# One decoder trunk on one core: the last token block's last 512 columns in two halves of 256, and the other blocks' output transfers issued by SP alone

## The chip, the cores and the metric

The kernel runs on one core of one Trainium2 chip. The metric is the device time of one execution in microseconds (us). Before the change three runs took 1270.3, 1270.86 and 1270.3 us, so the median is 1270.3 us. The execution that the profiler recorded took 1270.41 us by the same clock; the span in its trace, from the first to the last instruction, is 1268.6 us, so 1.8 us lie outside the trace.

## The reference: what is computed

Two layers over 512 tokens of 1024 numbers: a convolution module and a retention module, each followed by a feed-forward block with a short causal convolution. Everything is float32. What matters here is the very end:

```python
def conv_ffn(x, w_in, dw_w, dw_b, w_out):
    h = x @ w_in
    a, u = jnp.split(h, 2, axis=-1)
    a = causal_dwconv(a, dw_w, dw_b)
    return (jax.nn.silu(a) * u) @ w_out
...
        x = x + conv_ffn(h, ffn_w_in[i], ffn_dw_w[i], ffn_dw_b[i], ffn_w_out[i])
    return rmsnorm(x, final_g)
```

The last product, `@ w_out` of layer 1, gives 512 x 1024 numbers. They are added to the residual x, and each token's row is divided by the root of the mean of its 1024 squares and multiplied by the gain final_g. A token's scale is known only when its whole row is.

## The kernel before

**Precision.** A float32 product is made of three matmuls: each operand is split into a high part (rounded by ScalarE, line 238 or 384) and the rest (VectorE, lines 242 and 385), and `mm3` (lines 307 to 310) adds high by high, low by high and high by low in one PSUM bank. So lines 308, 309 and 310 carry the matmuls of nearly all stages; the tile names tell the stage.

**Order of work.** The layer's feed-forward block runs in four groups of hidden columns (line 30). For each group the hidden values `ys` are made first, and then they are multiplied by `w_out` (loop at line 1334). That second product is laid out with tokens on the partitions: for each half g of the 1024 output columns (g = 0 is columns 0 to 511, g = 1 is 512 to 1023) and each of the four blocks tb of 128 tokens, one PSUM bank `lo` takes 128 x 512 results. The last group has four hidden tiles (y_18 to y_21), so a bank of it takes 4 x 3 = 12 matmuls of 512 columns, and for g = 1 these come for all four tb in turn from one chunk of weights. A scheduler that works from a model of the engines sets the order of the instructions within each engine's queue; each engine then runs its queue strictly in order.

**The tail.** `finish` (line 1312) is called for each bank. In the last group it does, for block tb and half g:

- line 1318, VectorE: bank plus residual into `xT[2*tb+g]`;
- line 1321, ScalarE: the squares of it, with their sum per token into `ssq` (a second instruction reads the accumulator);
- for g = 0: line 1323, VectorE: sum/1024 + 1e-6; line 1324, GpSimd: the half is multiplied by the gain (`fgb[0]`, the tile `cos` reused);
- for g = 1: line 1327, VectorE: the two sums together into `fv`; line 1328 calls `rsqrt_small` (line 346), which raises `fv` to the power -0.5 on GpSimd (line 350) into `fr`; line 1329, ScalarE: the half g = 0 times `fr`; line 1330, ScalarE's queue: the output transfer of that half (128 rows of 2 KB, 256 KB); line 1331, VectorE: the half g = 1 times `fr` times the gain (the tile `sin`); line 1332, SP's queue: its output transfer (256 KB).

So there are eight output transfers, four issued by ScalarE and four by SP, all at the end. Below, C0 to C3 stand for line 1329 of blocks 0 to 3, M0 to M3 for line 1331, and Q3 for line 1321 of block 3 and g = 1.

`ssq` lives in the pool `sp` of small tiles. Pools lie one behind the other in SBUF, each tile rounded up to 32 bytes, so the pools opened after `sp` (the split activations and the working tiles of each stage) start where `sp` ends.

Of the kernel before, what the change touches and what calls it, by code (L numbers as in the profile page):

```python
# [9 lines left out]
F32 = mybir.dt.float32  # L10
F32R = mybir.dt.float32r
I32 = mybir.dt.int32
AF = mybir.ActivationFunctionType
ALU = mybir.AluOpType
PSUM = bass.MemoryType.PSUM

P = 128
D = 1024
S = 512
KD = D // P  # L20
NTB = S // P
# [134 lines left out]
def trunk(ctx, tc, xt_d, positions, ret_gn_g, final_g, weights_d, cols_d, mats_d, ident_d, decay_d, invf_d, out):  # L156
    nc = tc.nc
    pe, act, dve, pool = nc.tensor, nc.scalar, nc.vector, nc.gpsimd
# [3 lines left out]
    xp = ctx.enter_context(tc.tile_pool(name="xp", bufs=1))  # L162
    sp = ctx.enter_context(tc.tile_pool(name="sp", bufs=4))
# [6 lines left out]
    def psum(name):  # L170
        return pp.tile([P, S], F32, tag="ps", name=name)
# [135 lines left out]
    def mm3(ps, wh, wl, xh, xl, first, last, **check):  # L307
        pe.matmul(ps, wh, xh, start=first, stop=False, **check)  # L308
        pe.matmul(ps, wl, xh, start=False, stop=False, **check)  # L309
        pe.matmul(ps, wh, xl, start=False, stop=last, **check)  # L310
# [33 lines left out]
    xT = [xs_all[:, k, :] for k in range(KD)]  # L344
# [73 lines left out]
    QB = 32  # L418

    def blocks(t):  # L420

        return t.rearrange("p (a b q) -> p a b q", a=NTB, q=QB)
# [449 lines left out]
    N2 = S // 2  # L872
# [112 lines left out]
    def ffn_half(fp, l, norm, f0, f1, hooks=(), side=None, each=None):  # L985
        ys, wt, mid = [], {}, {}
        hooks = list(hooks)

        def mm(f):
            if f % 2 == 0:  # L990
                wt["a"] = weights()
                wt["u"] = weights()
            o = (f % 2) * P
            mid[f] = []
            for which in "au":
                ps = psum(f"f{which}{l}_{f}")
                for k in range(KD):
                    mm3(ps, *wt[which](k, o, o + P), *norm.xs[k], k == 0, k == KD - 1)
                mid[f].append(ps)
                hook = hooks.pop(0) if hooks else None  # L1000
                if hook:
                    hook()

        def evac(f):
            pa, pu = mid.pop(f)
            ap = fp.tile([P, S + 32], F32, tag="ap", bufs=2, name=f"ap{l}_{f}")[:, :2 + S]
            pool.memset(ap[:, :2], 0.0)
            dve.tensor_tensor(out=ap[:, 2:], in0=pa, in1=norm.rb, op=ALU.mult)  # L1008
            t = taps(fp, l, f, ap)
            scaled = pool.tensor_tensor(out=t, in0=t, in1=norm.rb, op=ALU.mult)  # L1010
            y = fp.tile([P, S], F32, tag="fy", bufs=2, name=f"fy{l}_{f}")
            product = dve.tensor_tensor(out=y, in0=pu, in1=t, op=ALU.mult)
            ys.append(split(y, f"y{l}_{f}", ("yh", "yl"), fp))
            if side is not None and f >= 2:
                with tc.issue_after(scaled.ins), tc.issue_after(product.ins):
                    next(side, None)

        mm(f0)
        for f in range(f0 + 1, f1):
            mm(f)  # L1020
            evac(f - 1)
            if each is not None:
                next(each, None)
        evac(f1 - 1)
        return ys

    with ExitStack() as es:
# [4 lines left out]
        def sums_of_x():  # L1032

            yield
            for k in range(4):
                left.sums_of(k)
                yield

        for n, (f0, f1, by_blocks) in enumerate(GROUPS[0]):
            if by_blocks:  # L1040
                ys = ffn_blocks(fp, 0, n1, f0, f1, left, rot)
            else:
                ys = ffn_half(fp, 0, n1, f0, f1, (None, n1.stats, n1.bcast), each=sums_of_x())
# [9 lines left out]
    with ExitStack() as es:  # L1053
# [191 lines left out]
        def ret_y(h, yt):  # L1245
            if h == H - 1:
                ys = []
                for e in range(4):
                    ps = psum(f"yt{h}{e}")
                    for i in range(NTB):  # L1250
                        pe.transpose(ps[:, i * P:(i + 1) * P], yt[i][:, e * P:(e + 1) * P], ident)
                    ys.append(split(ps, f"yt{h}{e}", ("yth", "ytl"), rt4))
                return ys
            return [split(yt[:, e], f"yt{h}{e}", ("yth", "ytl"), rt4) for e in range(4)]
# [3 lines left out]
        v = ret_vg(0, 0)  # L1258
# [11 lines left out]
        for h in range(1, H):  # L1270
            qk, ys = ret_qk(h, yt)
            proj_out(ys, f"ro{h - 1}", None, order=by_quarter, groups=(0,) if h == H - 1 else (0, 1))
            sc = ret_scores(h, qk, None)
            v, gg = ret_vg_blocks(h)
# [3 lines left out]
        ys = ret_y(H - 1, yt)  # L1278
# [4 lines left out]
    with ExitStack() as es:  # L1283
        fp = es.enter_context(tc.tile_pool(name="f1", reuse_waits="tile", bufs=6))
        lp = es.enter_context(tc.tile_pool(name="lp", reuse_waits="tile", bufs=1))
        xt = lp.tile([P, NTB, 4, KD * QB], F32, name="xt")
        sum_pool[0] = fp
        fgb = (cos, sin)
        for g in range(2):
            act.dma_start(fgb[g], final_g[512 * g:512 * (g + 1)].partition_broadcast(P))  # L1290
        lefts = []

        def between():


            xq = fp.tile([P, 4, NTB, KD, QB], F32, tag="sh", bufs=1, name="xq")
            for k in range(KD):
                dve.transpose(xq[:, :, :, k, :].rearrange("p c t q -> p t c q"), blocks(xT[k]))
            yield
            quarters(xt, xq.rearrange("p c t k q -> p c t (k q)"), nc.sync)  # L1300
            left = Factors(n3, list(n3.xs), fp, lambda name: fp.tile([P, 2, N2], F32, tag="fy", bufs=2, name=name), True)
            lefts.append(left)
            for k in range(4):
                left.sums_of(k)
                if k < 3:
                    yield
            for k in range(KD):
                left.normed_split(k)

        ssq = sp.tile([P, NTB, 2], F32, tag="ssq", bufs=1, name="ssq")  # L1310

        def finish(n, g, tb, ps):
            d = xt[:, tb].rearrange("p a (k q) -> p k a q", q=QB)[:, 4 * g:4 * g + 4]
            if n < len(GROUPS[1]) - 1:
                dve.tensor_tensor(out=d, in0=blocks(ps), in1=d, op=ALU.add)
                return
            dv, d = d, xT[2 * tb + g]
            dve.tensor_tensor(out=blocks(d), in0=blocks(ps), in1=dv, op=ALU.add)
            j = xp.tile([P, S], F32, tag="nsq", bufs=2, name=f"junk{tb}{g}")
            v = ssq[:, tb, g:g + 1]  # L1320
            act.activation(j, d, AF.Square, accum_out=v)
            if g == 0:
                dve.tensor_scalar(out=v, in0=v, scalar1=1.0 / D, scalar2=EPS, op0=ALU.mult, op1=ALU.add)
                pool.tensor_tensor(out=d, in0=d, in1=fgb[0], op=ALU.mult)
                return
            vv = sp.tile([P, 1], F32, tag="fv", name=f"fv{tb}")
            dve.tensor_scalar(out=vv, in0=v, scalar1=1.0 / D, scalar2=ssq[:, tb, 0:1], op0=ALU.mult, op1=ALU.add)
            r = rsqrt_small(vv, 1, f"fr{tb}")
            act.activation(xT[2 * tb], xT[2 * tb], AF.Copy, scale=r)
            nc.scalar.dma_start(out[0, tb * P:(tb + 1) * P, :512], xT[2 * tb])  # L1330
            dve.scalar_tensor_tensor(out=d, in0=d, scalar=r, in1=fgb[1], op0=ALU.mult, op1=ALU.mult)
            nc.sync.dma_start(out[0, tb * P:(tb + 1) * P, 512:], d)

        for n, (f0, f1, by_blocks) in enumerate(GROUPS[1]):
            if by_blocks:
                ys = ffn_blocks(fp, 1, n3, f0, f1, lefts[0])
            else:
                side = between()
                ys = ffn_half(fp, 1, n3, f0, f1, (None, n3.stats, n3.bcast), each=side)
                for _ in side:  # L1340
                    pass
            nk = len(ys)
            for g in range(2):
                last = n == len(GROUPS[1]) - 1 and g == 1
                ps = [psum(f"lo{n}{g}{tb}") for tb in range(NTB)]
                groups = []
                for k0, kn in _out_chunks(f0, f1, last):
                    groups += [(k0 + k, k, w) for w in [weights()] for k in range(kn)]
                    if last and k0 + kn < nk and k0 > 0:
                        continue  # L1350
                    for tb in range(NTB):
                        for f, k, w in groups:
                            yh, yl = ys[f]
                            mm3(ps[tb], yh[:, tb * P:(tb + 1) * P], yl[:, tb * P:(tb + 1) * P], *w(k, 0, 512),
                                f == 0, f == nk - 1)
                        if k0 + kn == nk:
                            finish(n, g, tb, ps[tb])
                    groups = []
# [79 lines left out]
```

## Time and profile before

| | |
|---|---|
| median of three runs | 1270.3 us |
| profiled execution | 1270.41 us |
| its span | 1268.6 us |
| instructions | 17818 |
| TensorE busy | 1257.9 us, 99% of the span |
| VectorE busy | 949.8 us, 75% |
| ScalarE busy | 617.5 us, 49% |
| GpSimd busy | 269.0 us, 21% |
| mean granted TensorE clock | 0.998 |
| output transfers of 256 KB | 4 on ScalarE's queue, 4 on SP's, median 3.1 us from issue to landing |

Times in the trace are in us from the span's start. PE is TensorE, PEld its weight load, DVE VectorE, ACT ScalarE, POOL GpSimd, SP the engine that only issues transfers; a name with q (ACTq, SPq) is that engine's queue issuing something. q1 is the hardware queue of the transfers that SP issues, q10 that of ScalarE's; both are served by the same 16 DMA engines. A row of the timeline gives start, duration, engine, line, what is written and read, and in brackets the idle time before it and what ended it. An instruction's duration includes its way through the pipeline, so the next may start on the same engine before it ends.

### The profile page before, as it was taken

The numbers are of one execution on the slowest core, as the hardware profiler recorded it, in microseconds if no ns is written. First come the engines' busy times: TensorE is split into PE (matmuls) and PEld (weight loads), VectorE is DVE, ScalarE is ACT, GpSimd is POOL, SyncE is SP. The second block draws the span as 40 slices with busy tenths as digits, with TensorE's granted clock in tenths as the row PEclk, the third lists the DMA queues.
The fourth block names the chain that finished last, engine by engine and source line by source line (L and its number), as shares of the span: only waits on it lengthen the run. The fifth ranks groups of instructions, "written<-read, shape, count | busy, mean of one in ns | idle before, by whom it ended". The sixth has DMA issues, their size and how long they took to land.

```text
span 1268.6 us, 17818 instructions
## 1 busy us (share of the span) xinstructions
PE 1257.9 (99%) x7035; PEld 1099.1 (87%) x7035; DVE 949.8 (75%) x1346; ACT 617.5 (49%) x900; POOL 269.0 (21%) x242
## 2 busy tenths in 40 slices
PE   9999999999999999999999999999999999999997
PEld 7889988888998998888888888878888899899896
DVE  6998757884796798589696696596879677577565
ACT  6646644442562665435335345344536256266354
POOL 0958321011101110221311412304312100010002
PEclk9999999999999999999999999999999999999999
DMA  8633332233655664313314404313152664565531
GB/s 328 237 126 108 112 120 77 103 121 100 175 158 133 184 151 164 116 67 108 108 42 154 135 27 166 116 74 134 67 149 86 160 170 143 140 169 153 128 100 67
DMA packets 38100, 164.26 MB, mean 129 GB/s; under 512 B 4992, under 2 KB 11904, under 8 KB 24192
## 3 DMA queue, kind: packets, MB, share of 16 engines
q1 hardware_dynamic: 27936, 134.01, 30.2%
q0 software_dynamic: 6480, 23.60, 10.2%
q10 hardware_dynamic: 3600, 5.52, 1.5%
q8 instruction: 55, 0.90, 0.3%
q14 instruction: 29, 0.24, 0.1%
HBM read 137.94 MB, written 2.10 MB: 110 GB/s over the span
## 4 chain that ended last, share of the span: by engine, by line
PE 95%; DVE 3%; issue 1%; POOL 1%; DMA 0%; ACT 0%; SPq 0%; POOLq 0%; DVEq 0%
PE fz L310 5%; PE fz L309 5%; PE fz L308 5%; PE fo L308 3%; PE fo L309 3%; PE fo L310 3%; PE lo L308 3%; PE lo L309 3%; PE lo L310 3%; PE cph L621 3%; PE qk L308 2%; PE qk L309 2%; PE qk L310 2%; PE fp L309 2%; PE fp L308 2%; PE fp L310 2%
## 5 line engine op out<-in xcount | busy, mean ns | idle before, releaser
L242 DVE TENSOR_TENSOR wl<-wr,wh 128x1024 fp32r<-128x1024 f32 (+2 forms) x272 | 334.0, 1233 | 143.5 <-ACT wh L238 140.8
L238 ACT CAST wh<-wr 128x1024 fp32r<-128x1024 f32 (+2 forms) x274 | 281.7, 1032 | 284.5 <-PE lo L309 49.3
L1116 POOL TENSOR_TENSOR gg<-gg,gn 128x512 f32<-128x512 f32 x16 | 27.5, 1721 | 179.3 <-ACT gg L1115 179.3
L670 DVE SCALAR_TENSOR_TENSOR tp<-hp,prm,tp 128x512 f32<-128x512 f32 x80 | 55.7, 745 | 0.4
L291 POOL DMA_DIRECT2D wr<-wr x15 | 13.1, 876 | 186.1 <-DVE fy L959 105.4
L661 POOL TENSOR_TENSOR pla<-pla,plt 128x512 f32<-128x512 f32 x36 | 49.1, 1366 | 9.7 <-ACT pla L657 5.6
L982 ACT ACTIVATE ft<-ft 128x512 f32<-128x512 f32 x44 | 27.5, 628 | 31.5 <-DVE ft L981 30.8
L980 DVE SCALAR_TENSOR_TENSOR ft<-ap,prm,ft 128x512 f32<-128x512 f32 x44 | 32.8, 746 | 10.4 <-ACT ft L979 10.4
L938 ACT COPY u<-fz 128x256 f32<-128x256 f32 x60 | 22.4, 373 | 35.4 <-PE fz L310 33.7
L1100 POOL TENSOR_TENSOR rs<-rs 128x512 f32<-128x512 f32 x16 | 24.8, 1561 | 67.4 <-DVE rs L1099 42.1
L979 ACT ACTIVATE ft<-ap,prm 128x512 f32<-128x512 f32 x44 | 35.9, 815 | 5.5 <-DVE ap L1008 4.5
L281 POOL DMA_DIRECT2D wr<-in_weights_dram x15 | 13.5, 898 | 113.2 <-DVE ws L280 61.4
L309 PE MATMUL fp<-n3sh,wl 128*128 128x256 f32 x128 | 36.2, 283 | 0.0
L308 PE MATMUL fp<-n3sh,wh 128*128 128x256 f32 x128 | 36.2, 283 | 0.0
L310 PE MATMUL fp<-n3sl,wh 128*128 128x256 f32 x128 | 36.2, 283 | 0.0
L309 PE MATMUL fz<-n3sh,wl 128*128 128x256 f32 x128 | 36.1, 283 | 0.0
L310 PE MATMUL fz<-n3sl,wh 128*128 128x256 f32 x128 | 36.1, 283 | 0.0
L308 PE MATMUL fz<-n3sh,wh 128*128 128x256 f32 x128 | 35.9, 283 | 0.0
L660 ACT ACTIVATE plt<-hp,prm 128x512 f32<-128x512 f32 x36 | 25.8, 723 | 20.6 <-POOL pla L661 20.2
L981 DVE SCALAR_TENSOR_TENSOR ft<-ap,prm,ft 128x512 f32<-128x512 f32 x44 | 33.8, 768 | 0.4
L466 DVE TENSOR_TENSOR xT<-ro,xT 128x512 f32<-128x512 f32 x32 | 21.6, 679 | 16.1 <-PE ro L310 16.1
L621 PEld LDWEIGHTS cph<-ph,cmat 128*128 128x128 f32 x288 | 32.6, 192 | 0.2
(2078 smaller groups left out, 4283.1 us busy)
## 6 DMA issues: line engine op xcount, KB each, us to landing
wr<-in_weights_dram SPq DMA_DIRECT2D x104, 1024.0 KB, 4.9
wr<-wr POOLq DMA_DIRECT2D x30, 512.0 KB, 4.6
cmat<-in_mats_dram SPq DMA_DIRECT2D x4, 2304.0 KB, 10.9
wr<-in_weights_dram POOLq DMA_DIRECT2D x15, 512.0 KB, 5.8
wr<-in_weights_dram SPq DMA_DIRECT2D x8, 512.0 KB, 3.6
xt<-xq SPq DMA_DIRECT2D x16, 128.0 KB, 5.9
wr<-in_weights_dram SPq DMA_DIRECT2D x6, 256.0 KB, 7.2
yt<-yq ACTq DMA_DIRECT2D x24, 64.0 KB, 2.1
```

The costliest lines, as they stand in the source:

```text
L238: latest[0] = act.copy(hi[:, o:o + n], raw[:, s + o:s + o + n])
L242: latest[1] = low_on.get(i, dve).tensor_tensor(out=lo[:, o:o + n], in0=raw[:, s + o:s + o + n], in1=hi[:, o:o + n].bitcast(F32), op=ALU.su ...
L308: pe.matmul(ps, wh, xh, start=first, stop=False, **check)
L309: pe.matmul(ps, wl, xh, start=False, stop=False, **check)
L310: pe.matmul(ps, wh, xl, start=False, stop=last, **check)
L621: pe.matmul(ps[:, g * P:(g + 1) * P], mats[i][g][:, s, :], ph[:, g, NSH - 1 - s:NSH - 1 - s + P], start=s == 0, stop=s == NSH - 1)
L661: gate[0] = pool.tensor_tensor(out=pl, in0=pl, in1=tm, op=ALU.add).ins
L670: dve.scalar_tensor_tensor(out=a, in0=hp[:, t:t + S], scalar=tap(t, i), in1=a, op0=ALU.mult, op1=ALU.add)
L979: act.activation(t, ap[:, 2:2 + S], AF.Identity, scale=wc(2), bias=wc(3))
L980: dve.scalar_tensor_tensor(out=t, in0=ap[:, 1:1 + S], scalar=wc(1), in1=t, op0=ALU.mult, op1=ALU.add)
L981: dve.scalar_tensor_tensor(out=t, in0=ap[:, 0:S], scalar=wc(0), in1=t, op0=ALU.mult, op1=ALU.add)
L982: act.activation(t, t, AF.Silu)
```

## The change

For block tb = 3 and g = 1 of the last group, the 12 matmuls of 512 columns become 12 of 256 columns into one bank and 12 of 256 columns into a new bank `lolast`, and `finish` is called after each. For the first half it adds the residual, squares 256 columns and adds their sum into `ssq[:, tb, 0:1]`; for the second half it does the same with the other 256 columns, and then the rest of the tail as before on all 512. `ssq` grows from 2 to 3 columns per block. The transfer of line 1330 is issued by SP for blocks 0 to 2 and by ScalarE for block 3 only.

```diff
-        ssq = sp.tile([P, NTB, 2], F32, tag="ssq", bufs=1, name="ssq")
-
-        def finish(n, g, tb, ps):
+        ssq = sp.tile([P, NTB, 3], F32, tag="ssq", bufs=1, name="ssq")
+
+        def finish(n, g, tb, ps, half=None):
...
             dv, d = d, xT[2 * tb + g]
-            dve.tensor_tensor(out=blocks(d), in0=blocks(ps), in1=dv, op=ALU.add)
-            j = xp.tile([P, S], F32, tag="nsq", bufs=2, name=f"junk{tb}{g}")
-            v = ssq[:, tb, g:g + 1]
-            act.activation(j, d, AF.Square, accum_out=v)
+            if half is None:
+                v = ssq[:, tb, g:g + 1]
+                dve.tensor_tensor(out=blocks(d), in0=blocks(ps), in1=dv, op=ALU.add)
+                j = xp.tile([P, S], F32, tag="nsq", bufs=2, name=f"junk{tb}{g}")
+                act.activation(j, d, AF.Square, accum_out=v)
+            else:
+                c = slice(half * N2, half * N2 + N2)
+                dve.tensor_tensor(out=blocks(d)[:, 2 * half:2 * half + 2], in0=ps.rearrange("p (a b q) -> p a b q", a=2, q=QB),
+                                  in1=dv[:, 2 * half:2 * half + 2], op=ALU.add)
+                j = xp.tile([P, N2], F32, tag="nsq", bufs=2, name=f"junk{tb}{g}{half}")
+                v = ssq[:, tb, 1 + half:2 + half]
+                act.activation(j, d[:, c], AF.Square, accum_out=v)
+                if half == 0:
+                    dve.tensor_scalar(out=ssq[:, tb, 0:1], in0=v, scalar1=1.0 / D, scalar2=ssq[:, tb, 0:1], op0=ALU.mult,
+                                      op1=ALU.add)
+                    return
...
-            nc.scalar.dma_start(out[0, tb * P:(tb + 1) * P, :512], xT[2 * tb])
+            (nc.sync if half is None else nc.scalar).dma_start(out[0, tb * P:(tb + 1) * P, :512], xT[2 * tb])
...
                     for tb in range(NTB):
+                        if last and k0 == 0 and kn == nk and tb == NTB - 1:
+                            for half, p in enumerate((ps[tb], psum("lolast"))):
+                                for f, k, w in groups:
+                                    t = slice(tb * P, (tb + 1) * P)
+                                    mm3(p[:, :N2], ys[f][0][:, t], ys[f][1][:, t], *w(k, half * N2, half * N2 + N2),
+                                        f == 0, f == nk - 1)
+                                finish(n, g, tb, p[:, :N2], half)
+                            continue
                         for f, k, w in groups:
```

## The prediction

> **What bounds the kernel now.** I read the page first, for what the span is made of.
>
> ```profile
> span 1268.6 us, 17818 instructions
> ```
> ```profile
> PE 1257.9 (99%) x7035; PEld 1099.1 (87%) x7035; DVE 949.8 (75%) x1346; ACT 617.5 (49%) x900; POOL 269.0 (21%) x242
> ```
>
> TensorE is busy almost throughout, but the change touches only what follows its last dozen matmuls, and there another limit holds. So I read next the timeline of the tail, from the scaling of block 0 to the last transfer.
>
> ```profile
> 1259.67 0.72 ACT L1329 ACTIVATE xT<-xT,fr0y 128x512 f32<-128x512 f32 x1 [0.20 <-POOL fr0y L350]
> 1259.68 0.75 DVE L1331 SCALAR_TENSOR_TENSOR xT<-xT,fr0y,sin 128x512 f32<-128x512 f32 x1
> ...
> 1260.25 0.39 PE L310 MATMUL lo<-wl,y_21h 128*128 128x512 f32 x1
> 1260.31 0.70 ACT L1329 ACTIVATE xT<-xT,fr1y 128x512 f32<-128x512 f32 x1
> 1260.35 0.74 DVE L1331 SCALAR_TENSOR_TENSOR xT<-xT,fr1y,sin 128x512 f32<-128x512 f32 x1
> 1260.43 0.39 ACTq L1330 DMA_DIRECT2D out_dram<-xT  x1
> 1260.46 4.52 SPq L1332 DMA_DIRECT2D out_dram<-xT  x4
> 1260.92 0.70 ACT L1329 ACTIVATE xT<-xT,fr2y 128x512 f32<-128x512 f32 x1
> 1261.01 0.68 DVE L1318 TENSOR_TENSOR xT<-lo,xt 128x512 f32<-128x512 f32 x1
> 1261.04 1.15 ACTq L1330 DMA_DIRECT2D out_dram<-xT  x2
> 1261.61 0.74 DVE L1331 SCALAR_TENSOR_TENSOR xT<-xT,fr2y,sin 128x512 f32<-128x512 f32 x1
> 1262.24 0.63 ACT L1321 ACTIVATE junk<-xT 128x512 f32<-128x512 f32 x1 [0.62 <-DVE xT L1318]
> ...
> 1263.87 0.75 DVE L1331 SCALAR_TENSOR_TENSOR xT<-xT,fr3y,sin 128x512 f32<-128x512 f32 x1 [0.66 <-POOL fr3y L350]
> 1264.62 0.37 ACTq L1330 DMA_DIRECT2D out_dram<-xT  x1
> ```
>
> Two things are to be seen. First the arithmetic of block 3: TensorE ends at 1260.25 + 0.39 = 1260.64; the add waits for VectorE until 1261.01 and is done at 1261.69; yet its squares (Q3) start only at 1262.24. ScalarE was not computing then: its queue was issuing the transfer of block 2 (the pair of issues runs from 1261.04 to 1262.19). So an issue on ScalarE's queue holds back the block that ends last, by 1262.24 - 1261.69 = 0.55 us. That is what the change takes away. Second, the transfers start when block 0 is scaled (1260.43 and 1260.46), not when block 3 is.
>
> So the third view is the DMA engines' share, in stretches cut where it changes.
>
> ```profile
> core 0: us, PE busy (x) PEld busy (x) DVE busy (x) ACT busy (x) POOL busy (x), PEclk, DMA share, GB/s
> 1261.25:1261.50 0.25, 0.00 (x0) 0.00 (x0) 0.25 (x1) 0.25 (x1) 0.00 (x0) 1.00 0.73 287
> 1261.50:1265.25 3.75, 0.00 (x0) 0.00 (x0) 1.82 (x4) 1.57 (x4) 0.54 (x1) 0.80 1.00 379
> 1265.25:1265.50 0.25, 0.00 (x0) 0.00 (x0) 0.00 (x0) 0.00 (x0) 0.00 (x0) 0.50 0.93 311
> 1265.50:1266.75 1.25, 0.00 (x0) 0.00 (x0) 0.00 (x0) 0.00 (x0) 0.00 (x0) 0.50 1.00 382
> 1266.75:1267.00 0.25, 0.00 (x0) 0.00 (x0) 0.00 (x0) 0.00 (x0) 0.00 (x0) 0.50 0.57 205
> ```
>
> From about 1261.32 (0.73 of a slice) to 1266.89 (0.57 of one) the 16 engines are busy without a gap: eight transfers of 256 KB, 2.10 MB in 5.57 us, 0.70 us each. The first byte comes 0.89 us after the first issue, and the span ends 1.71 us after the last byte, with nothing but landing and the closing steps in it. So the end is: block 0 ready, 0.89 us, eight transfers back to back, 1.71 us. Block 3 does not set it: its transfers, issued at 1264.62, can begin at 1264.62 + 0.89 = 1265.51, and the six before them end at 1261.32 + 6 x 0.70 = 1265.5. They arrive just in time; all that their lateness can have cost is the dip in one slice, 0.25 x (1 - 311/382) = 0.05 us.
>
> What sets block 0? The chain of work in order of time goes there by GpSimd.
>
> ```profile
> 1252.52 0.70 DVE xT L1318
> ...
> 1254.05 5.05 POOL xT L1324 x4
> 1259.11 0.54 POOL fr0y L350
> ```
>
> GpSimd's four gain multiplications of the g = 0 halves (5.05 us) stand ahead of block 0's rsqrt in its queue. The change touches none of these.
>
> **The change part by part.** The prices of narrow instructions come from other stages.
>
> ```profile
> 1239.46 0.42 DVE L967 TENSOR_TENSOR fy<-fp,u 128x256 f32<-128x256 f32 x1 [0.32 <-PE fp L310]
> ```
> ```profile
> L938 ACT COPY u<-fz 128x256 f32<-128x256 f32 x60 | 22.4, 373 | 35.4 <-PE fz L310 33.7
> ```
> ```profile
> 1212.87 0.36 PE fz L308 x3
> ...
> 1251.12 0.68 PE lo L308 x3
> ```
> ```profile
> L1332 SPq DMA_DIRECT2D out_dram<-xT x4: 333/336/348, 1260.5 to 1264.6; - x4
> ```
>
> *Matmuls.* 12 of 512 columns at 0.68/3 = 0.227 us become 24 of 256 at 0.12: 2.88 - 2.72 = +0.16 us on TensorE. The second half ends at 1260.80, the first 12 x 0.12 = 1.44 us earlier, at 1259.36. The other bank costs nothing: `lolast` takes that of block 0, g = 0, empty since the add at 1252.52.
>
> *VectorE.* The first half's add (0.42) can start at 1259.36, ahead of M0 (1259.68), or behind it. Ahead, it has M0 and block 2's `fv` queued behind it: M0 moves to about 1259.95, M1 with it. M0's transfer is the second in the stream and has until 1261.3 + 0.7 - 0.89 = 1261.1 to be issued; M0 would end at 1260.7. Hidden. The extra sum into `ssq` works on one column, less than 0.42 by the same row, and block 3 waits for it last.
>
> *ScalarE.* One square of 512 becomes two of 256, 0.37 each, the first ready at about 1259.8. C0 is ready at 1259.67, so by readiness C0 stays first, and C1 and C2 follow it as now. I take the cost to the first transfer as 0; the other order is a rival below.
>
> *The transfers moved to SP.* Each takes SP 0.336 us against 0.70 us of the engines' time, so six in a row (2.0 us) stay ahead of the data. SP's queue holds nothing else then, but in it each transfer waits behind the one of the half before; C0 to C2 and M0 to M2 come in that order anyway. First issue: C0's end, 1260.4, as before.
>
> A single queue could also feed the engines worse than two. The nearest rows are of weight loading at the start, which SP's queue does alone:
>
> ```profile
> q1 hardware_dynamic: 823, 2.48, 104.5%
> ```
>
> That is full occupancy, 2.48 MB in the 6 us from 14 to 20, or 413 GB/s, with mostly larger pieces and in the other direction. At 413 the 2.10 MB would take 5.08 us, 0.49 less; for the other bound I take as much again, +0.5, and use 0, since occupancy is full in both.
>
> On this the Trainium skill (*DMA: Bandwidth & Descriptors*, section "Issuing engines are not separate DMA queues") says that transfers of all issuing engines run on the same 16 DMA engines, and that issuing from several saves only the issuing time. The trace agrees (no gap with either one queue or two); the rule speaks against the move only in that three issues, 3 x 0.336 = 1.0 us, are no longer made in parallel, and by it the sum would stay as it is, since the data are slower than the issues.
>
> *Block 3's arithmetic.* M0 and M1 start 0.67 apart, so with them as above VectorE is free at about 1261.3; the second half's add ends at 1261.7. From Q3's start to M3's it is 1263.87 - 1262.24 = 1.63 us now, and 0.63 - 0.37 less with the narrow square, 1.37; M3 takes 0.75: 1263.8 instead of 1264.62, about 0.8 us earlier. If M2 goes ahead of that add, 0.67 of it is lost. What hides this gain is the stream: the six transfers occupy the engines until 1265.5 in any case.
>
> *Sum.* First transfer unmoved, 0; dip filled, -0.05; queue, 0. The profiled execution, 1270.41 us, becomes 1270.36; the median of the runs shown is 0.11 lower than that execution, so **1270.3 us**: no change. A change under 0.2%, about 2.5 us, can hardly be told from none by a measurement of this kernel.
>
> **The rivals.**
>
> *The arithmetic of block 3 sets the end.* For it: it is what ends last on the engines, and the transfers have 0.0 us in hand by my own count. Against: the stream has no gap. If it were so, the end would move by up to the 0.8 us above and a single queue no slower: 1270.3 - 0.8 = 1269.5. A queue at 413 GB/s would give 1269.8.
>
> *Slower: the first square is queued ahead of C0 on ScalarE.* The scheduler fixes the order by its model, and the two are ready within 0.15 us of each other (1259.67 and 1259.8). Then C0 starts at about 1260.2, and the first issue and the whole stream shift by 0.5: 1270.8. It decides as soon as the model has block 0's rsqrt end after the first half's add. Slower queue service (+0.5 at most) would look the same in the time, but with gaps in the share.
>
> *Slower by more: the layout.* `ssq` grows from 32 to 48 bytes, 64 when rounded, so all pools behind it, with the split activations and the working tiles of every stage, start 32 bytes later than the tiles they meet. No row shows such a shift as a whole; the nearest are two instructions that differ by one step of 4 bytes in one input.
>
> ```profile
> L980 DVE SCALAR_TENSOR_TENSOR ft<-ap,prm,ft 128x512 f32<-128x512 f32 x44 | 32.8, 746 | 10.4 <-ACT ft L979 10.4
> ...
> L981 DVE SCALAR_TENSOR_TENSOR ft<-ap,prm,ft 128x512 f32<-128x512 f32 x44 | 33.8, 768 | 0.4
> ```
>
> 22 ns in 746, 3%, on VectorE. It costs nothing while TensorE is the limit; if 0.3% of it reached TensorE's 1257.9 us, that would be 3.8 us, 1274. The sign is open. I take 0.
>
> *The halves don't finish apart.* The scheduler may interleave the two banks' matmuls; then block 3 is ready 0.16 us later than before instead of earlier, and its transfers leave a gap of that size, less the 0.55 us won on ScalarE: no change.
>
> **How the numbers follow.** Forecast (stream unmoved) 0.50; arithmetic or faster queue 0.12; C0 or the queue later 0.20; halves interleaved 0.05; layout 0.13, of which 0.04 faster and 0.09 slower by over 0.2%. All but the last lie within 0.2%: same 0.87, faster 0.04, slower 0.09. The range takes in 1269.5 and 1270.8 and the scatter of the runs: 1269.2 to 1271.3. Only the layout is left outside.
>
> **What would show it.** Right: gapless DMA share from about 1261.3 to 1266.9, Q3's two squares ended well before 1262.9, the last issues near 1263.8, the same span. Wrong: a first issue moved from 1260.4 (the order on ScalarE), a share under 0.95 (the queue), or pitches or waits changed before 1250 (the layout). A span shorter by over 0.3 us with the stream's start unmoved would overturn the claim that the transfers bound the end.

## The result and the profile after

The changed kernel takes 1284.83 us (median of 4 runs, 1284.67 to 1285.09) against 1270.43 us before: the ratio is 1.0113, 95% interval 1.0101 to 1.0124. It is 14.4 us slower, where no change was forecast and the range ended at 1271.3.

The page after shows a longer span and TensorE busy for all of it; the other engines are busy almost as long as before.

```profile
span 1283.3 us, 17851 instructions
...
PE 1273.7 (99%) x7047; PEld 1092.7 (85%) x7047; DVE 951.0 (74%) x1348; ACT 619.1 (48%) x902; POOL 269.7 (21%) x242
```

Is it the tail, which is all that the diff seems to touch? The timeline of the tail after gives the first add of the last group on VectorE (`finish`, now line 1320), the first transfer on SP's queue and the last on ScalarE's.

```profile
1267.26 1.89 DVE L1320 TENSOR_TENSOR xT<-lo,xt 128x512 f32<-128x512 f32 x3 [5.75 <-PE lo L310]
...
1275.19 0.35 SPq L1342 DMA_DIRECT2D out_dram<-xT  x1
...
1279.00 0.39 ACTq L1342 DMA_DIRECT2D out_dram<-xT  x1
```

Before, that add started at 1252.52, the first transfer was issued 7.91 us later, and the span ended 8.17 us after that. Now it is 7.93 and 8.11 us. The tail kept its length; the add itself comes 14.74 us later, and the span grew by 14.7. So all of the loss lies ahead of the tail, in stages where both kernels compute with the same instructions in the same order on every engine.

Stretches cut at the same times show how fast TensorE goes there. The columns are those of the prediction's view of the DMA share; the figure in brackets behind the first of them, PE, is the number of matmuls. First before, then after:

```profile
500.00:800.00 300.00, 300.00 (x1346) 249.25 (x1345) 222.01 (x296) 129.41 (x177) 68.75 (x47) 1.00 0.31 106
```
```profile
500.00:800.00 300.00, 300.00 (x1312) 242.86 (x1311) 219.63 (x289) 126.88 (x173) 60.31 (x41) 1.00 0.31 101
```

TensorE is busy through all 300 us in both and the granted clock is 1.00 in both, but it does 1312 matmuls where it did 1346: 2.5% fewer. Single instructions tell more. The rows for a group of matmuls with 512 columns give shortest, median and longest duration in ns; the row for 256 columns gives the group's busy time in us and the mean duration in ns. Before, for the last product (`lo`), the retention's inner product (`o`) and a product of 256 columns:

```profile
L310 PE MATMUL lo<-wl,y_18h x8: 389/389/397, 1236.1 to 1258.2; 128*128 128x512 f32 x8
```
```profile
L308 PE MATMUL o<-v00h,sch x4: 389/389/389, 602.1 to 606.2; 128*128 128x512 f32 x4
```
```profile
L309 PE MATMUL fp<-n3sh,wl 128*128 128x256 f32 x128 | 36.2, 283 | 0.0
```

And after:

```profile
L310 PE MATMUL lo<-wl,y_18h x4: 396/396/397, 1250.7 to 1257.7; 128*128 128x512 f32 x4
```
```profile
L308 PE MATMUL o<-v00h,sch x4: 389/389/395, 609.6 to 613.7; 128*128 128x512 f32 x4
```
```profile
L309 PE MATMUL fp<-n3sh,wl 128*128 128x256 f32 x128 | 35.7, 279 | 0.0
```

The same matmul of 512 columns takes 396 ns instead of 389 in `lo`, still 389 in `o`, and one of 256 columns takes 279 instead of 283. What tells these apart is where the operands lie. A matmul has a standing operand, the 128 x 128 that are loaded into TensorE ahead of it, and a streaming one, the 512 or 256 columns that pass through. In `lo` and `fp` one operand is a weight (`wh`, `wl`, in the pool `wp` ahead of `sp`) and the other an activation (in a pool behind `sp`); in `o` both lie behind `sp`. Only the distance between the first kind's operands was changed by the 32 bytes by which `ssq` grew.

Taking the time from each matmul's start to the next (pauses over 0.32 us left out) and grouping by stage, I get 3636 matmuls of 512 columns in stages that became slower, by 6.3 ns on average, and 2710 of 256 in stages that became faster, by 2.8 ns: +22.8 - 7.6 = +15.2 us, against the 14.7 measured. The sum closes to 0.5 us without the tail.

### The profile page after: what moved, and what is told of

The parts are those of the page before. It is cut to its first block, busy times and chain, and to the rows that moved or that the text cites. A ratio compares the mean times of both kernels' runs of the same rounds, so it can differ in the third digit from the quotient of the medians.

```text
span 1283.3 us, 17851 instructions
## 1 busy us (share of the span) xinstructions
PE 1273.7 (99%) x7047; PEld 1092.7 (85%) x7047; DVE 951.0 (74%) x1348; ACT 619.1 (48%) x902; POOL 269.7 (21%) x242
## 4 chain that ended last, share of the span: by engine, by line
PE 97%; DVE 1%; POOL 1%; issue 0%; ACT 0%; POOLq 0%
PE fz L310 4%; PE fz L308 4%; PE fz L309 4%; PE fo L308 3%; PE fo L309 3%; PE fo L310 3%; PE lo L308 3%; PE lo L309 3%; PE lo L310 3%; PE cph L621 3%; PE qk L308 2%; PE qk L309 2%; PE qk L310 2%; PE ro L308 2%; PE ro L309 2%; PE ro L310 2%
```

## The experiments

The theories: **D**, the distance between the two operands of a matmul, in bytes within a partition, sets how fast it streams; **A**, the absolute place of the activations does; **T**, the change itself (the halves, the narrow instructions, the issues on SP) costs the time somewhere. D and A are the layout rival of the prediction made definite; T is all that the prediction priced.

**The change without the shift.** `sp` opens with a tile `pad` that nothing uses. Shortening it by as much as `ssq` grew puts every pool back:

```diff
-    sp.tile([P, 3 * LINE // 16], F32, tag="pad", bufs=1, name="pad")
+    sp.tile([P, 3 * LINE // 16 - 8], F32, tag="pad", bufs=1, name="pad")
```

> The changed kernel with the unused pad tile of the pool sp shortened by 8 numbers (32 bytes), so that every pool behind ssq lies where it lay before the change. Theory D (distance): the 32 bytes by which the activations moved against the weights cost 6.6 ns on each matmul of 512 columns between the two groups of pools and win 2.8 ns on each of 256. With the distance restored the starts are 0.227 and 0.120 us apart again and the time is that of the tail's change alone, for which the forecast still stands: 1269.5 to 1270.9, 1270.3 likeliest. Theory T (the split of the last block, its narrow instructions or the issues on SP cost the time somewhere): it stays at 1284.8.

Measured: 1270.38 us against 1270.68 for the kernel before beside it, ratio 0.9998 (0.9989 to 1.0007). T falls: the changed tail costs nothing and wins nothing that can be measured. The loss goes with the shift.

**The shift without the change.** The kernel before, with the pad 8 numbers longer:

```diff
-    sp.tile([P, 3 * LINE // 16], F32, tag="pad", bufs=1, name="pad")
+    sp.tile([P, 3 * LINE // 16 + 8], F32, tag="pad", bufs=1, name="pad")
```

> The kernel before with nothing but the pad tile lengthened by 8 numbers (32 bytes). Theory D: 1284.5 to 1285.2, with 0.233 us between starts at 512 columns and 0.117 at 256 in all stages whose operands lie on both sides of sp. Theory T: 1270.4, since no instruction differs from before.

Measured: 1285.15 us, ratio 1.0114 (1.0099 to 1.0130), with 0.2333 us between starts in `fo`, `lo`, `ro` and `vg` and 0.117 in `fp`. In the stretch from 500 to 800 us it does the same number of matmuls as the changed kernel, to the last one:

```profile
500.00:800.00 300.00, 300.00 (x1312) 242.84 (x1311) 219.27 (x288) 126.56 (x173) 60.30 (x41) 1.00 0.31 101
```

**Distance or place.** Eight unused numbers at the head of the first pool move weights and activations alike:

```diff
+    cp.tile([P, 8], F32, name="cpad")
     ones = cp.tile([P, P], F32, name="ones")
```

> The kernel before with 8 unused numbers at the head of the first pool: weights, residual and activations all lie 32 bytes later, their distance from one another is that of before. Theory D (distance between the two operands): 1270.4, starts 0.227 and 0.120 apart. Theory A (absolute place: activations that start at 128 bytes past a multiple of 256 are read more slowly than at 96): 1284.8 or worse, as weights move to 128 too.

Measured: 1270.72 us, ratio 1.0001 (0.9992 to 1.0010). A falls: the activations lie exactly where they lie in the slow kernel, and the time is the fast one's. Together with e2_shift32 this shows that the distance between the tiles ahead of `sp` and those behind it makes the whole loss.

```profile
500.00:800.00 300.00, 300.00 (x1346) 249.28 (x1345) 222.03 (x296) 129.44 (x177) 68.51 (x47) 1.00 0.32 106
```

One thing these runs leave open is which weight load the distance is to be taken to: the matmul's own standing operand, or that of the next matmul, whose load starts 2 to 4 ns after the matmul's own start and lasts 188 ns, so within the stream. Inside a stage both lie at the same remainder. Where stages meet, the records of the kernel before and of e2_shift32 point both ways. The four matmuls of `o` that are followed by one with a weight from `wp` take 235 ns to the next start in place of 227, though their own two operands kept their distance; and the three of `ro` that are followed by one of `sc`, which has no operand in `wp`, stay at 226 to 227, though theirs changed. Both speak for the next load. But of the nine matmuls of `lo` that are followed by one of `fz`, whose standing weight lies in `wp` like the streaming one of `lo`, six go from 226 or 227 to 233 or 236 (the others stay at 233), which speaks for the own operand. Below, the distance is that to the own operand.

**Other distances.** The pad 16, 24 and 32 numbers longer, and left out:

> The kernel before with the pad tile lengthened by 16 numbers: activations 64 bytes further from the weights. Theory D with a period of 64 bytes: 1270.4. With a cost that depends on the distance in some longer period: another time than 1270.4, near 1284.8 if 32 and 64 are alike. Theory A: 160 past a multiple of 256 is 32 past one of 64, as 96 is, so 1270.4 if the period is 64.

> The kernel before with the pad tile lengthened by 24 numbers: activations 96 bytes further from the weights. At 64 the two kinds of matmul came apart: 0.229 us between starts where the activations stream and the weights stand (fo, ro, fa, qk), 0.233 where it is the other way round (lo, vg), so the sign of the distance counts. If the cost repeats every 128 bytes, 96 is -32 for the first kind and +32 for the second: 0.233 and 0.233, 0.117 at 256 columns, 1285. If it repeats every 256 bytes, this shows two new points, +96 and -96, and the time lies between 1265 and 1290.

> The kernel before with the pad tile lengthened by 32 numbers: 128 bytes further. If the cost repeats every 128 bytes: 0.227 in all stages, 1270.4. If every 256: both kinds of matmul sit at the same point, so fo and lo agree with one another, at a value that no run has shown yet.

> The kernel before without the pad tile: activations 192 bytes nearer to the weights, which is the same place in a period of 256 bytes as 64 further. Period 256 (or 64, 128): as with 64 further, 1276.3, fo 0.229, lo 0.233. If the distance itself counts and not its remainder: another time.

Measured: 64 bytes further 1276.26 us (ratio 1.0043, 1.0028 to 1.0058), 96 further 1293.29 (1.0178, 1.0148 to 1.0207), 128 further 1288.93 (1.0144, 1.0114 to 1.0173), and without the pad, 192 nearer, 1276.50 (1.0045, 1.0026 to 1.0065). A period of 64 falls with the first. One of 128 falls with the second, for which it gave 1285, and with the third, which is not 1270.4. The second also lies above the 1290 that e5_shift96 gave as the upper end for a period of 256: its matmuls of 256 columns went back to 120.0 ns while those of 512 stayed slow. Left out and 64 further agree to 0.1 ns in every stage that meets the weights, and 128 further gives `fo` and `lo` nearly the same, 233.0 and 232.6, so 256 bytes is the period as far as this shows. In the stretch from 500 to 800 us, 64 further and then without the pad:

```profile
500.00:800.00 300.00, 300.00 (x1324) 244.88 (x1323) 220.06 (x293) 125.92 (x171) 65.24 (x44) 1.00 0.31 104
```
```profile
500.00:800.00 300.00, 300.00 (x1324) 244.88 (x1323) 220.08 (x293) 125.95 (x171) 65.29 (x44) 1.00 0.32 104
```

**Is the end set by the stream of transfers?** This tests the prediction's account of the tail, on the kernel of e1_padback. The transfers of columns 0 to 511 of blocks 0 to 2 are left out:

```diff
-            (nc.sync if half is None else nc.scalar).dma_start(out[0, tb * P:(tb + 1) * P, :512], xT[2 * tb])
+            if half is not None:
+                nc.scalar.dma_start(out[0, tb * P:(tb + 1) * P, :512], xT[2 * tb])
```

> The changed kernel with the pad shortened as in e1_padback, and without the output transfers of columns 0 to 511 of blocks 0 to 2, which leaves that part of the output unwritten. Theory S (the stream of output transfers sets the end of the tail, block 3's arithmetic is hidden): five transfers instead of eight; block 3's last issue, 11.6 us after the tail's first add as in e1_padback, then sets the end with 0.9 us to its first byte, two transfers of 0.7 us and 1.75 us: 268.9 - 1.0 or so, that is a span of 1267.9 (1267.5 to 1268.2 with the scatter of the start), shorter by about 1.0 us. Theory B (block 3's arithmetic sets the end already): the span stays at 1268.9.

Measured: 1269.51 us against 1270.54 (ratio 0.9989, 0.9978 to 1.0001), which is inconclusive as a time, but the span is 1268.2 against 1268.9 in e1_padback, at the upper end of the expectation; over all runs of the two the median span is 1267.7 against 1268.6 (the kernel before, run beside each, took 1270.54 and 1270.68). The DMA share shows what the time can't. In e1_padback, eight transfers:

```profile
1260.75:1261.50 0.75, 0.37 (x4) 0.17 (x2) 0.75 (x2) 0.75 (x3) 0.58 (x1) 1.00 0.00 0
1261.50:1261.75 0.25, 0.00 (x0) 0.00 (x0) 0.25 (x2) 0.25 (x2) 0.00 (x0) 1.00 0.48 188
1261.75:1267.00 5.25, 0.00 (x0) 0.00 (x0) 1.92 (x5) 1.73 (x4) 0.54 (x1) 0.90 1.02 380
1267.00:1267.25 0.25, 0.00 (x0) 0.00 (x0) 0.00 (x0) 0.00 (x0) 0.00 (x0) 0.50 0.62 213
```

No gap from 1261.63 (0.48 of a slice) to 1267.16 (0.62 of one). With five transfers there is a long one ahead of block 3's two, from 1264.5 to 1265.4 (0.37 of the last slice):

```profile
1263.50:1264.50 1.00, 0.00 (x0) 0.00 (x0) 0.71 (x1) 0.71 (x1) 0.26 (x1) 0.55 0.68 262
1264.50:1265.00 0.50, 0.00 (x0) 0.00 (x0) 0.04 (x1) 0.01 (x1) 0.00 (x0) 0.50 0.00 0
1265.00:1265.25 0.25, 0.00 (x0) 0.00 (x0) 0.00 (x0) 0.00 (x0) 0.00 (x0) 0.50 0.00 0
1265.25:1265.50 0.25, 0.00 (x0) 0.00 (x0) 0.00 (x0) 0.00 (x0) 0.00 (x0) 0.50 0.37 147
```

Three transfers, 2.1 us of the engines' time, are gone and the span is 0.7 us shorter, since now block 3's arithmetic is what the last transfers wait for. With all eight it is hidden.

**A better distance, tile by tile.** At 256 columns the distance of before is among the slow ones. Four of the seven products of a pair of hidden tiles in the feed-forward stages stream the sums `sh` and `sl`, which no matmul of 512 columns reads there. They can be moved alone, in both stages (shown for the first, where a second pad of 64 - 48 numbers behind the sums puts all else back; in the second a pad ahead of them is enough):

```diff
         fp = es.enter_context(tc.tile_pool(name="f0", reuse_waits="tile", bufs=8))
+        fp.tile([P, 48], F32, tag="spad", bufs=1, name="spad0")
...
         left = Factors(n1, list(n1.xs), fp, lambda name: fp.tile([P, 2, N2], F32, tag="fy", bufs=2, name=name))
+        fp.tile([P, 16], F32, tag="tpad", bufs=1, name="tpad0")
```

> The kernel of e1_padback (the changed tail, the pools at their old distance), with one thing moved: in both feed-forward stages only the tiles of the factors' sums (sh, sl) lie 32 bytes later, all else where it lay. Theory D holds tile by tile, and at 256 columns 32 bytes are better than 0: 4 of the 7 products of a pair of hidden tiles stream these sums, 15 pairs x 4 x 24 = 1440 matmuls, each 2.7 ns less (0.120 to 0.117 us): 3.9 us less than 1270.4, 1266.5 (1265.8 to 1267.2). Matmuls of 512 columns stay at 0.227. If the distance of whole pools counts, or the gain at 256 columns came from the weight load of neighbouring matmuls, it stays at 1270.4.

> As e9_sums32, with the sums 192 bytes later (64 nearer, in a period of 256). A point that no run has shown at 256 columns. Where the sign counts as at 512 columns, this is another value than the 117.6 ns of 64 later; between 115.7 and 120.0 ns, that is 1264.2 to 1270.4.

> As e9_sums32, with the sums 224 bytes later (32 nearer). At 512 columns 32 nearer and 32 further cost the same, 0.2333; if that symmetry holds at 256, this gives 1266.5 as e9_sums32 does; between 1264.2 and 1270.4.

> As e10_sums192, with the sums 160 bytes later (96 nearer), the last of the eight steps of 32 bytes at 256 columns. At 192 later the streams of the sums started 0.1139 us apart, at 224 later 0.1183. If 192 is the best place, this lies above 1260.9; if the cost falls further towards 160, below 1260.9. If a step of 32 that is odd is always worse than its even neighbour (32, 96 and 224 against 64 and 192), it lies between 1264 and 1270.4.

Measured, sums 32 bytes later: 1267.29 us (ratio 0.9974, 0.9963 to 0.9985), just above the upper end of the expectation, since the streams of the sums start 117.9 ns apart and not 117.3 (2.7 less than 120.0). 192 later: **1260.94 us** (0.9924, 0.9908 to 0.9939), 9.8 us below the kernel before and 23.9 below the changed one. 224 later: 1267.94 (0.9978, 0.9969 to 0.9988). 160 later: 1266.47 (0.9966, 0.9955 to 0.9978). Both neighbours of 192 lie above it. By the table below 192 is then the best of the eight steps for this case, though at 64, 96 and 128 the sums were never moved alone. The lower bounds given for e10_sums192, 1264.2 us and 115.7 ns, were too high. The sums' matmuls, 192 bytes later, as single instructions (283 before):

```profile
L309 PE MATMUL fp<-n3sh,wl 128*128 128x256 f32 x128 | 35.5, 277 | 0.0
```

The times from start to start over all these runs, by the remainder mod 256 of the streaming operand's place minus the standing one's, in ns. At 512 columns 0 to 128 are the stage `fo`, where activations stream, and 160 to 224 the stage `lo`, where weights do and the distance turns round; at 256 columns they are the pools moved as a whole (`fp`) up to 128 and the sums moved alone (all their matmuls, in `fz` and `fp`) from 160 on. Each is a mean. At one remainder the groups of a stage still differ, at 32 from 114.1 ns (`fx<-n3n4h,wh`) to 119.1 (`fx<-n1n4h,wh`), so other things count as well:

| remainder, bytes | 0 | 32 | 64 | 96 | 128 | 160 | 192 | 224 |
|---|---|---|---|---|---|---|---|---|
| 512 columns | 226.9 | 233.3 | 228.9 | 233.4 | 233.0 | 234.1 | 233.3 | 233.3 |
| 256 columns | 120.0 | 117.1 | 117.6 | 120.0 | 119.2 | 117.5 | 113.9 | 118.3 |

## Why the prediction was wrong

The step that failed is the third rival, "the layout", which the text described and then set to 0. Its premise was right: all pools behind `ssq` moved by 32 bytes against the tiles that they meet. Its own sign came true as well, pitches that change before 1250. Three things in its working were not right.

- It took its price from VectorE (22 ns in 746) and let TensorE off: "It costs nothing while TensorE is the limit". TensorE itself reads both of those tiles. VectorE's busy time is 951.0 us after and 949.8 before; TensorE's matmuls of 512 columns went from 0.2269 to 0.2333 us apart, 2.8%.
- Its size, "if 0.3% of it reached TensorE's 1257.9 us, that would be 3.8 us", had no row behind it. The share is 2.8% on the 512-column matmuls and -2.4% on the 256-column ones, and the sum is the +14.7 us measured.
- It got a chance of 0.13 and lay outside the range by choice. No row of the trace before could have priced it: weights and activations lie at the same remainder there (96 mod 256), so no pair of that kind is seen at another distance. But the kernel held a hint that the layout matters, the tile `pad` that nothing uses: without it the kernel takes 1276.50 us (e7_nopad). A cost without a nearby row should have kept its whole size in the range, and its bound should have been sought on the engine with no slack.

On this the Trainium skill (*TensorE: Matmul & The Clock Gate*, section "Back-to-back issue gap") gives the isolated time from one matmul to the next by the number of columns alone, 518 cycles for 512 and 262 for 256 at 2.4 GHz, an estimate of 216 and 109 ns; for a sustained stream with weight loads it gives about 131 ns at 512. The runs here show 227 to 234 and 114 to 120 for the same instructions, by where the operands lie. The same skill (*SBUF — State Buffer*, section "Who interferes with whom") calls TensorE's two read ports, for the streaming operand and the weight load, independent, and says that TensorE never waits on anyone. By that rule the distance between them should not matter, and here it does, while moving both together costs nothing (e2_shift32 against e3_all32); the measurement decides. Why the distance counts, the runs don't show, and it stays open: the weight loads last 188 ns in both, only the streams lengthen.

The tail, with the layout put back (e1_padback), came out as worked out, with two sizes off. Times in e1_padback are 0.33 us later than before from the tail's first add on:

- *First transfer unmoved*: it is issued 7.91 us after the tail's first add in both (1260.76 - 1252.85 in e1_padback). C0 stays ahead of the first square on ScalarE, as forecast.
- *One queue feeds the engines as well as two*: with seven of the eight transfers on SP's queue, from 1261.63 to 1267.16 is 5.53 us, against 5.57. The issues on SP last up to 0.59 us instead of 0.336, still under the 0.70 of a transfer.
- *Block 3 earlier by about 0.8*: its last issue comes 11.59 us after that first add (1264.44 - 1252.85), 12.10 before: 0.51. The wait behind a transfer on ScalarE, 0.55 us, was replaced by one behind C2, which the working left out: the add of the second half is done at 1261.93, its squares start at 1262.27, at the end of C2 (1261.65 + 0.71 = 1262.36).

```profile
1261.51 0.42 DVE L1325 TENSOR_TENSOR xT<-lolast,xt 128x256 f32<-128x256 f32 x1
1261.65 0.71 ACT L1341 ACTIVATE xT<-xT,fr2y 128x512 f32<-128x512 f32 x1
...
1262.27 0.40 ACT L1329 ACTIVATE junk<-xT 128x256 f32<-128x256 f32 x1
```

- *The gain is hidden by the stream*: shown by the gapless share, and by the gap that opens with fewer transfers. The other rivals, block 3 setting the end, C0 late and the halves interleaved, did not occur.

## What to carry to other kernels

When a diff changes the size of any tile, however small, list which pools lie behind it and which matmuls then have one operand on each side; hold the layout fixed with a pad before judging the rest of the change. If TensorE is busy throughout and the time moves, count the matmuls in the same stretch of both traces before looking at the part of the code that was edited. Time saved on arithmetic that a gapless stream of transfers hides was worth nothing here (block 3 0.51 us earlier, the same time); what counted was when the stream starts and how many bytes it has.

## What the runs showed of the hardware that was not expected

- With the instructions unchanged, the mean time from one float32r matmul to the next depends on the distance in bytes between its streaming operand and the standing ones. It was seen in steps of 32 bytes and, as far as tested, with a period of 256: 226.9 to 234.1 ns at 512 columns, 113.9 to 120.0 at 256. Whether the own standing operand counts or the one loaded during the stream is open.
- The best distance differs: 0 at 512 columns, 192 at 256. At 512 columns 64 and 192 differ (228.9 and 233.3), so it matters which of the two lies further, or which of them streams: in these runs both change together, though at 0 and 128 `fo` and `lo` are alike within 0.5 ns.
- The kernel with the sums at 192 is the fastest of all that ran, 1260.94 us; the distances of the other 256-column products, which share their tiles with products of 512 columns, were not tried apart.
